# Stick-breaking attention by parts: the running product weighs differences of neighbouring value rows

## The chip, the cores and the metric

The kernel runs on one core of one Trainium2 chip. The metric is the device time of one execution in microseconds, lower is better. A core has a matrix engine (PE, with its weight loads shown apart as PEld), a vector engine (DVE), a scalar engine (ACT), a general engine (POOL) and an engine that here only issues DMAs (SP). PE, DVE, ACT and POOL each take their own instructions in a fixed order and wait for one another by semaphores. SBUF is the on-chip memory of tiles; PSUM is the small memory that matmuls write to. POOL works on SBUF alone.

## The reference, cut to what matters

One layer of a residual trunk: 2048 positions of width 1024. A combined projection gives four heads of differential attention and eight heads of stick-breaking attention, then an output projection and a SwiGLU feed-forward part follow. The change concerns the stick-breaking heads (width 64):

```python
z = jnp.einsum('bqhd,bkhd->bhqk', qb, k).astype(jnp.float32) * scale
mask = (k_pos[None, :] < q_pos[:, None])[None, None]
log_1mb = jnp.where(mask, jax.nn.log_sigmoid(-z), 0.0)
rem = lax.cumsum(log_1mb, axis=3, reverse=True) - log_1mb
a = jnp.where(mask, jnp.exp(jax.nn.log_sigmoid(z) + rem), 0.0)
return jnp.einsum('bhqk,bkhd->bqhd', a.astype(v.dtype), v)
```

For query t and key s < t the weight is sigmoid(z_ts) times the product, over the keys j between s and t, of sigmoid(-z_tj). Write C_s for the product of sigmoid(-z_tj) over s <= j < t, and C_t = 1. Since sigmoid(z) = 1 - sigmoid(-z), the weight is C_(s+1) - C_s.

## The kernel before

The whole kernel is one function, `block`. Work is in tiles of 128 positions (16 of them, index `i` for queries, `t` for the projection). Eight head groups run one after the other: `g` 0 to 3 are the differential heads (`diff_attn`), `g` 4 to 7 hold two stick-breaking heads each (`sb_attn`, map `m` 0 and 1). While the attention of one group runs, the projection of the next is made beside it (`proj_stream`, `advance`); beside group 7, which has no next group, runs the output projection (`out_proj`). The feed-forward part comes last.

A stick-breaking stage (`stage_a`) is one query tile, one head and one block `b` of up to 1024 keys, blocks from right to left. It takes two SBUF tiles of the pool `z4` (nine buffers, line 265): `be` for the weights and `om` for the running product. Per chunk of up to 512 keys, from right to left, these things happen:

- PE writes scores into a PSUM tile `sc` (four buffers; line 507). On the diagonal chunk one more matmul adds the mask (line 509), through a constant `tri` whose upper part is -1e38.
- ACT makes sigmoid(-z) into `om` (line 619) and sigmoid(z) into `be` or back into `sc` (line 620).
- DVE scans `om` in place from right to left, a running product that starts from 8192 or from the carry of the chunk to the right (line 622). The scan takes a second input, which its second operation passes by: the PSUM tile `sc`.
- The product of sigmoid(z) with the scan shifted by one key goes to `be` (line 623): on DVE with one input in PSUM, or, for the chunk `c == 1` of groups 4 to 6, on POOL (`aside`).

Then `split_t` (line 450) makes two 16-bit parts of the stage's weights, the high part by a cast on ACT (`to16`, line 89) and the rest by a subtraction on POOL (`tt`, line 98), and a DMA transposes both into `aT`. Some stages later (`PD`, `lag`) PE multiplies `aT` with the value rows (`pv`, line 518), three matmuls of 64 columns for each 128 keys, and accumulates in PSUM (`yp`). `finish` normalises and stores.

Values come from the projection. In groups 4 to 6 (`turned`) two tiles at a time are projected into two PSUM banks of the pool `psj`, which has two, and `split_psum` (lines 358 to 364) makes 16-bit high and low parts of the values in `v`, the high part on ACT or DVE by whichever has less noted load, the low part on DVE. Group 7 does the same tile by tile in `proj_out`.

The order of instructions on each engine is fixed when the program is built, by a scheduler that goes by priorities (`PRI`) and by what each instruction needs; nothing in the change touches its tables.

Of the kernel before, what the change touches and what calls it, by code (L numbers as in the profile page):

```python
# [11 lines left out]
F32 = mybir.dt.float32  # L12
# [17 lines left out]
HIDDEN = -1.0e38  # L30
# [29 lines left out]
def block(tc, a, out):  # L60
# [3 lines left out]
    with top:  # L64
# [54 lines left out]
        id16 = cp.tile([P, P], F16, name="id16")  # L119
        DVE.tensor_copy(id16[:], id32[:])  # L120
        idb = cp.tile([P, P], BF16, name="idb")
        DVE.tensor_copy(idb[:], id32[:])
        tri = cp.tile([P, P], BF16, name="tri")
        DVE.memset(tri[:], 0.0)
        POOL.affine_select(tri[:], tri[:], pattern=[[-1, P]], compare_op=ALU.is_gt, fill=HIDDEN, base=0, channel_multiplier=1)
# [131 lines left out]
        with ExitStack() as ph1:  # L257
# [4 lines left out]
            bias = s16p.tile([P, 4, 256], F32, name="bias", bufs=1)  # L262

# [21 lines left out]
            def load_w(g, st=None):  # L285
# [24 lines left out]
                else:  # L310
                    G["epsy"], G["kz"], G["nkz"] = c1(), c1(), c1()
                    DVE.tensor_scalar(G["epsy"][:], t2[:], EPS * 2.0 ** 28, 1e-37, op0=ALU.mult, op1=ALU.max)
                    times(kap, kap, kap)
                    DVE.tensor_scalar(G["kz"][:], kap[:], 2.0 ** -9, 2.0 ** -110, op0=ALU.mult, op1=ALU.max)
                    DVE.tensor_scalar(G["nkz"][:], G["kz"][:], -1.0, None, op0=ALU.mult)
                G["q"], G["k"], G["v"] = [], [], []
# [29 lines left out]
            def turned_out(pq, pv, qT, kT, v, j):  # L346
# [8 lines left out]
                vv = v[:, two, :].rearrange("p t (h s e) -> p t h s e", h=2, s=2)  # L355
                split_psum(vv[:, :, :, 0, :], vv[:, :, :, 1, :], pv[:, :256].rearrange("p (t h e) -> p t h e", t=2, h=2), 256)

            def split_psum(hi, lo, src, n):
                sc = 2.0 ** -11
                if pick(A=0.84 * n + 60, D=1.05 * n + 70) == "A":  # L360
                    ACT.mul(hi, src, sc)
                else:
                    DVE.tensor_scalar(hi, src, sc, None, op0=ALU.mult)
                DVE.scalar_tensor_tensor(lo, src, sc, hi, op0=ALU.mult, op1=ALU.subtract)  # L364
                note("D", 1.05 * n + 70)

            @pri("po")
            def proj_out(g, G, pj, B, j):
                st, v, raw = B
                nv = 1 if g < 4 else 2  # L370
                vv = v[:, j, :].rearrange("p (h s e) -> p h s e", h=nv, s=2)
                split_psum(vv[:, :, 0, :], vv[:, :, 1, :], pj[:, 256:384].rearrange("p (h e) -> p h e", h=nv), 128)
                if g < 4:
                    if pick(A=270, D=335) == "A":
# [3 lines left out]
                else:  # L378
                    split_psum(st[:, 0:4, j, 0, :], st[:, 0:4, j, 1, :], pj[:, :256].rearrange("p (c e) -> p c e", c=4), 256)

# [36 lines left out]
            def proj(g, G, fresh=None):  # L417
                for t in range(NT):
# [6 lines left out]
                    if t % 4 == 0:  # L425
                        v = sp.tile([P, 4, 256], F16, tag="v", bufs=KB, name=nm("v"))
                    if turned(g):
# [8 lines left out]
                        if t % 2 == 1:  # L436
                            turned_out(pq, pv_, qT, kT, v, t % 4)
# [6 lines left out]
                    proj_out(g, G, pj, (st, v, raw), t % 4)  # L444
# [59 lines left out]
            def score_chunk(G, sc, i, q, m, w, cut=False, turned=False):  # L504
# [3 lines left out]
                if cut:  # L508
                    last = PE.matmul(sc[:, 128 * w - P : 128 * w], lhsT=idb[:], rhs=tri[:], start=False, stop=True, skip_group_check=True)
# [3 lines left out]
            def pv(G, yp, y0, aT, b, n, o, wd, start, stop):  # L513
                nb = n // P
                for j in range(nb):
                    v = G["v"][2 * b + j // 4][:, j % 4, :]
# [79 lines left out]
            def sb_attn(g, G):  # L596
# [6 lines left out]
                def stage_a(i, m, b):  # L603
                    L = (i + 1) * 128
                    n = min(1024, L - 1024 * b)
                    be, om = z4(), z4()
                    if b == i // 8:
                        DVE.memset(om[:, n : n + 1], 8192.0)
                    else:
                        DVE.tensor_copy(om[:, n : n + 1], last[m][:, 0:1])  # L610
# [735 lines left out]
```

## Time and profile before

| what | value |
|---|---|
| three timed runs | 2677.06, 2681.61, 2683.46 us (median 2681.61) |
| span of the profiled execution | 2680.8 us (its own time is shown by this span alone) |
| differential groups 0 to 3, up to the first scan | 0 to 604 us |
| stick-breaking groups 4, 5, 6, first scan to last | 604 to 764, 764 to 923, 923 to 1094 us |
| stick-breaking group 7 with the output projection | 1094 to 1354 us |
| rest of the output projection | 1354 to 1427 us |
| feed-forward part | 1427 us to the end |

The profile is one execution on the chip. For a group of instructions it names the line, the engine, the operation, what is written and read, the count, the busy time and mean duration, and after a second bar the idle time of the engine just before them with what ended it. PE's busy time counts each matmul from issue to its last result, so matmuls overlap in it; the spacing of matmuls in a row tells what one costs.

### The profile page before, as it was taken

The page shows a single profiled execution, that of the slowest core. Times are in us where ns is not written, and L with a number is a line of the kernel's source. Part 1 is how long each engine was busy: PE and PEld are TensorE (multiplying, and loading weights), DVE is VectorE, ACT ScalarE, POOL GpSimd, SP SyncE. Part 2 cuts the span into 40 slices and gives each one's busy share as a digit, 9 for nine tenths or more (in the row PEclk, how much of TensorE's full clock was granted, in tenths as well). Part 3 has the DMA queues.
Part 4 walks back from the last instruction along what each step waited for, and adds up shares of the span by engine and source line. Part 5 has one row for each costly group of instructions (what it writes and reads, how often), then busy time and mean ns, then how long its engine had stood idle before and what let it go on. Part 6 is the DMA issues. An engine that isn't in the chain of part 4 may idle for free. (4 is left out here: it accounts for less than half of the span.)

```text
span 2680.8 us, 50579 instructions
## 1 busy us (share of the span) xinstructions
PE 2492.4 (93%) x19628; PEld 1498.6 (56%) x19628; DVE 1932.7 (72%) x3711; ACT 1347.0 (50%) x2487; POOL 1489.1 (56%) x1098
## 2 busy tenths in 40 slices
PE   6998989888988989889989899999999999999999
PEld 4655656577776776557775344444444444444444
DVE  6898969898989989877766868777685544444434
ACT  4665656567978878665644535344352112111121
POOL 2578667667767766546764656565564232322323
PEclk9999999999999999999999899999999999999999
DMA  6777697767998979987897574665649743635532
GB/s 222 213 162 181 146 200 168 179 143 184 193 179 179 185 160 209 210 191 217 218 285 282 208 250 178 255 226 202 245 183 346 293 177 143 233 141 186 195 111 95
DMA packets 619585, 534.41 MB, mean 199 GB/s; under 512 B 480640, under 2 KB 548224, under 8 KB 609104
## 3 DMA queue, kind: packets, MB, share of 16 engines
q1 hardware_dynamic: 617520, 529.09, 69.9%
q8 instruction: 154, 2.52, 0.4%
q0 software_dynamic: 512, 1.36, 0.2%
q14 instruction: 87, 0.71, 0.1%
q10 hardware_dynamic: 1312, 0.72, 0.1%
HBM read 261.08 MB, written 147.32 MB: 152 GB/s over the span
## 5 line engine op out<-in xcount | busy, mean ns | idle before, releaser
L98 POOL TENSOR_TENSOR s<-z,s 128x1024 f16<-128x1024 f32 (+7 forms) x288 | 472.0, 1647 | 142.5 <-ACT s L89 109.8
L507 PE MATMUL sc<-kT,qT 128*128 128x512 f16 (+3 forms) x1520 | 382.0, 353 | 53.3 <-DVE z L623 19.3
L622 DVE TENSOR_TENSOR_SCAN z<-z,sc 128x512 f32<-128x512 f32 (+3 forms) x320 | 352.8, 1112 | 58.6 <-ACT sc L620 38.0
L1138 PE MATMUL pd<-wd,act 128*128 128x512 f16 x1764 | 390.9, 379 | 1.2 <-DVE cg L1071 1.2
L326 PE MATMUL pj<-w,xt 128*128 128x384 f16 x1920 | 352.2, 331 | 18.8 <-ACT xt L683 6.9
L1030 PEld LDWEIGHTS <-wg 128*128 128x128 f16 x1848 | 182.0, 99 | 230.2 <-issue 16.4
L518 PE MATMUL yp<-v,aT 128*128 128x64 f16 (+1 forms) x4896 | 269.8, 204 | 41.6 <-DMA aT<-s 40.2
L518 PEld LDWEIGHTS <-aT 128*128 128x128 f16 x4896 | 237.5, 99 | 120.4 <-DMA aT<-s 52.5
L1030 PEld LDWEIGHTS <-wu 128*128 128x128 f16 x1848 | 180.7, 98 | 218.0 <-issue 2.6
L98 POOL TENSOR_TENSOR act<-cg,act 128x512 f16<-128x512 f32 x112 | 148.5, 1337 | 262.9 <-ACT act L1097 150.8
L1138 PEld LDWEIGHTS <-act 128*128 128x128 f16 x1764 | 172.8, 98 | 209.4 <-issue 2.8
L326 PEld LDWEIGHTS <-xt 128*128 128x128 f16 x1920 | 187.3, 99 | 147.5 <-issue 21.4
L89 ACT CAST s<-z 128x128 f16<-128x128 f32 (+7 forms) x215 | 173.1, 809 | 134.1 <-DMA aT<-s 40.5
L98 POOL TENSOR_TENSOR hs<-hs,cu 128x512 f32<-128x512 f32 x99 | 130.9, 1328 | 171.3 <-DVE hs L1144 70.8
L619 ACT ACTIVATE z<-sc,c 128x512 f32<-128x512 f32 (+3 forms) x320 | 210.7, 663 | 25.6 <-PE sc L507 11.7
L1097 ACT CAST act<-cg 128x512 f16<-128x512 f32 x126 | 77.3, 616 | 238.4 <-DVE cg L1103 162.7
L507 PEld LDWEIGHTS <-qT 128*128 128x128 f16 x1520 | 128.4, 99 | 121.0 <-DVE z L623 23.0
L832 PE MATMUL po<-wo,mt 128*128 128x256 f16 x1536 | 180.7, 277 | 13.9 <-DVE xf L835 8.4
L1030 PE MATMUL pm<-X,wu 128*128 128x512 f16 x792 | 180.4, 379 | 1.3 <-DVE wu L221 1.3
L1030 PE MATMUL pm<-X,wg 128*128 128x512 f16 x792 | 181.3, 382 | 0.0
L342 PE MATMUL pj<-xt,w 128*128 128x128 f16 x2304 | 175.0, 220 | 6.7 <-DVE v L364 5.7
L1144 DVE SCALAR_TENSOR_TENSOR hs<-pd,c,hs 128x512 f32<-128x512 f32 x136 | 99.0, 747 | 109.6 <-PE pd L1138 83.1
(266 smaller groups left out, 4737.6 us busy)
## 6 DMA issues: line engine op xcount, KB each, us to landing
xt<-xs SPq DMA_DIRECT2D x112, 512.0 KB, 4.3
hs<-hd SPq DMA_DIRECT2D x68, 512.0 KB, 4.5
hd<-hs SPq DMA_DIRECT2D x56, 512.0 KB, 4.7
split<-wg SPq DMA_DIRECT2D x11, 1792.0 KB, 7.8
split<-wu SPq DMA_DIRECT2D x11, 1792.0 KB, 6.7
split<-wd SPq DMA_DIRECT2D x11, 1792.0 KB, 7.2
wg<-split SPq DMA_DIRECT2D x11, 1792.0 KB, 7.3
wd<-split SPq DMA_DIRECT2D x11, 1792.0 KB, 12.2
```

Of the source, the lines that this page charges most:

```text
L89: ACT.copy(dst, src)
L98: (DVE if e == "D" else POOL).tensor_tensor(dst, a_, b_, op)
L326: PE.matmul(pj[:, :384], lhsT=xv[:, xi, kt, :], rhs=G["w"][:, wi, kt, :], start=n == 0, stop=n == 23)
L342: PE.matmul(o, lhsT=x_ if c == 2 else w_, rhs=w_ if c == 2 else x_, start=n == 0, stop=n == 23)
L507: last = PE.matmul(sc[:, : 128 * w].rearrange("p (t n) -> p t n", n=P), lhsT=G["q"][i // 4][:, a_, i % 4, :], rhs=G["k"][q][:, b_, 0:w, :] ...
L518: PE.matmul(yp[:, y0 : y0 + wd], lhsT=aT[:, a_, :], rhs=v[:, v_ : v_ + wd], start=start and j == 0 and q == 0, stop=stop and j == nb - 1 a ...
L619: ACT.activation(om[:, lo:hi], sc[:, :w], AF.Sigmoid, scale=G["nkz"][:])
L622: DVE.tensor_tensor_scan(ov, ov, sc[:, :w], om[:, hi : hi + 1], op0=ALU.mult, op1=ALU.bypass)
L832: PE.matmul(po[:, sl], lhsT=mt[:, kt, P * xi : P * xi + P], rhs=wos[2 * h + n][wi][:, kt, :], start=q == 0, stop=q == 23)
L1030: front[0] = PE.matmul(ps_[:].rearrange("p (t n) -> p t n", n=P), lhsT=wv[:, wo, wi, 128 * kt : 128 * kt + 128], rhs=X[xo][:, :, xi, kt, : ...
L1138: front[0] = PE.matmul(po[:], lhsT=act[:, ao, xi, 128 * j : 128 * j + 128], rhs=W["d"][:, wo, wi, :], start=start and u == 0 and q == 0, s ...
L1144: DVE.scalar_tensor_tensor(dst, po[:], kd[:], src, op0=ALU.mult, op1=ALU.add)
```

## The change

The sum over keys of (C_(s+1) - C_s) v_s is taken by parts: it is v_t plus the sum over s <= t of C_s (v_(s-1) - v_s), where in the kernel's scaling 8192 stands for 1. So the running product itself becomes the weight, and what it weighs is the difference of neighbouring value rows.

- The second sigmoid, the product with the shifted scan, the mask matmul and the carry column go. Only query tile `i == 0` keeps the old way, with raw values.
- On the diagonal chunk the scan multiplies and adds: its second input is a constant `diag`, zero but for 8192 on the diagonal, which starts the running product anew there. On other chunks the second input is `om` itself, passed by as before. The carry is a column of the neighbouring `om`.
- `steps_out` is new. It splits the projected values into 16-bit parts in a `z4` tile (`G["r"]`, two tiles per group, eight tiles of positions each), makes the differences with matmuls against the constants `dif` and `edge` into the same PSUM bank, and splits those into `v`.
- `stage_c` adds 8192 times the row's own value with two matmuls against the constant `idc`.

```diff
-                G["q"], G["k"], G["v"] = [], [], []
+                G["q"], G["k"], G["v"], G["r"] = [], [], [], []
...
-                vv = v[:, two, :].rearrange("p t (h s e) -> p t h s e", h=2, s=2)
-                split_psum(vv[:, :, :, 0, :], vv[:, :, :, 1, :], pv[:, :256].rearrange("p (t h e) -> p t h e", t=2, h=2), 256)
-
-            def split_psum(hi, lo, src, n):
-                sc = 2.0 ** -11
+                steps_out(G, pv, 256, 2, v, t)
...
+            def steps_out(G, pv, o, k, v, t):
+                t0 = t + 1 - k
+                r = t0 % 8
+                rv = G["r"][t // 8][:].bitcast(F16)[:, 256 * r : 256 * (r + k)].rearrange("p (t h s e) -> p t h s e", t=k, h=2, s=2)
+                split_psum(rv[:, :, :, 0, :], rv[:, :, :, 1, :], pv[:, o - P * k : o].rearrange("p (t h e) -> p t h e", t=k, h=2), P * k)
+                d = pv[:, o : o + P * k].rearrange("p (t h e) -> p t h e", t=k, h=2)
+                PE.matmul(d, lhsT=dif[:], rhs=rv[:, :, :, 1, :], start=True, stop=False, skip_group_check=True)
+                for u in range(max(t0, 1), t + 1):
+                    for s in range(2):
+                        PE.matmul(d[:, u - t0], lhsT=edge[:], rhs=raw_v(G, u - 1)[:, :, s, :], start=False, stop=False, skip_group_check=True)
+                PE.matmul(d, lhsT=dif[:], rhs=rv[:, :, :, 0, :], start=False, stop=True, skip_group_check=True)
+                vv = v[:, t0 % 4 : t0 % 4 + k, :].rearrange("p t (h s e) -> p t h s e", h=2, s=2)
+                split_psum(vv[:, :, :, 0, :], vv[:, :, :, 1, :], d, P * k, 1.0)
...
-                if cut:
-                    last = PE.matmul(sc[:, 128 * w - P : 128 * w], lhsT=idb[:], rhs=tri[:], start=False, stop=True, skip_group_check=True)
...
-                    be, om = z4(), z4()
-                    if b == i // 8:
-                        DVE.memset(om[:, n : n + 1], 8192.0)
-                    else:
-                        DVE.tensor_copy(om[:, n : n + 1], last[m][:, 0:1])
+                    om = z4()
+                    carry = 0.0 if b == i // 8 else last[m][:, 0:1]
...
-                        aside = c == 1 and turned(g)
-                        beta = be[:, lo:hi] if aside else sc[:, :w]
-                        ACT.activation(om[:, lo:hi], sc[:, :w], AF.Sigmoid, scale=G["nkz"][:])
-                        ACT.activation(beta, sc[:, :w], AF.Sigmoid, scale=G["kz"][:])
                         ov = om[:, lo:hi][:, ::-1]
-                        DVE.tensor_tensor_scan(ov, ov, sc[:, :w], om[:, hi : hi + 1], op0=ALU.mult, op1=ALU.bypass)
-                        (POOL if aside else DVE).tensor_tensor(be[:, lo:hi], beta, om[:, lo + 1 : hi + 1], ALU.mult)
+                        ACT.activation(om[:, lo:hi], sc[:, :w], AF.Sigmoid, scale=G["nkz"])
+                        DVE.tensor_tensor_scan(ov, ov, diag[:, 512 - w :][:, ::-1] if cut else ov, carry, op0=ALU.mult, op1=ALU.add if cut else ALU.bypass)
+                        carry = om[:, lo : lo + 1]
...
-                    return n, split_t(be[:, :n], n, "A", "P", wide[0] if g < NG - 2 else None)
+                    return n, split_t(om[:, :n], n, "A", "P", wide[0] if g < NG - 2 else None)
...
+                    if b == 0 and i > 0:
+                        for s in range(2):
+                            PE.matmul(yp[:, y0 : y0 + 64], lhsT=idc[:], rhs=raw_v(G, i)[:, m, s, :], start=False, stop=r == k - 1 and m == 1 and s == 1, skip_group_check=True)
```

What stands on DVE in group 5 for the left key block of query tile 14 shows the scans. Before (line 622 is the scan, 623 the product, 494 a part of `finish`; `z` are the `z4` tiles, `sc` the score banks):

```order
L622 SCALAR_TENSOR_TENSOR z_14308<-z_14308,sc_14310 128x512
L622 SCALAR_TENSOR_TENSOR z_14308<-z_14308,sc_14318 128x512
L623 TENSOR_TENSOR z_14307<-sc_14318,z_14308 128x512
L622 SCALAR_TENSOR_TENSOR z_14356<-z_14356,sc_14358 128x512
L494 SCALAR_TENSOR_TENSOR mo_14013<-yp_13017,c_269,mo_14013 128x4x128
L608 MEMSET z_14523 128x1
L622 SCALAR_TENSOR_TENSOR z_14356<-z_14356,sc_14366 128x512
L623 TENSOR_TENSOR z_14355<-sc_14366,z_14356 128x512
```

The same place on DVE with the change (the scan is line 638 now; 510 is a part of `finish`):

```order
L638 SCALAR_TENSOR_TENSOR z_13910<-z_13910,diag 128x384
L638 SCALAR_TENSOR_TENSOR z_13910<-z_13910 128x512
L638 SCALAR_TENSOR_TENSOR z_14033<-z_14033,z_13877 128x512
L638 SCALAR_TENSOR_TENSOR z_14033<-z_14033 128x512
L638 SCALAR_TENSOR_TENSOR z_14077<-z_14077,z_13910 128x512
L510 TENSOR_TENSOR y_13737<-yp_12812,yrs_13741 128x512
L638 SCALAR_TENSOR_TENSOR z_14077<-z_14077 128x512
```

The products are gone, scans follow one another, and no scan names a score bank any more: what it reads is its own tile, `diag`, or a neighbour's carry column.

On POOL the same stages stood like this before (line 623 is the product set aside, line 98 the low part of the 16-bit split):

```order
L623 TENSOR_TENSOR z_14307<-z_14307,z_14308 128x512
L623 TENSOR_TENSOR z_14355<-z_14355,z_14356 128x512
L98 TENSOR_TENSOR s_14199<-z_14179,s_14199 128x896
L98 TENSOR_TENSOR s_14326<-z_14307,s_14326 128x1024
L623 TENSOR_TENSOR z_14479<-z_14479,z_14480 128x512
```

And with the change:

```order
L98 TENSOR_TENSOR s_13890<-z_13877,s_13890 128x896
L98 TENSOR_TENSOR s_13923<-z_13910,s_13923 128x896
L98 TENSOR_TENSOR s_14046<-z_14033,s_14046 128x1024
L98 TENSOR_TENSOR s_14090<-z_14077,s_14090 128x1024
L98 TENSOR_TENSOR s_14216<-z_14203,s_14216 128x1024
```

POOL's row of splits is unbroken now; each split still needs the whole scan of its stage and its cast.

68 lines of the change are left out of this document (43 added, 25 removed).

## The prediction

> **What bounds the kernel now.** I read the page's first two parts, then the table of stages, then the groups of one stage, and last single tiles and stretches of time.
>
> ```profile
> span 2680.8 us, 50579 instructions
> PE 2492.4 (93%) x19628; PEld 1498.6 (56%) x19628; DVE 1932.7 (72%) x3711; ACT 1347.0 (50%) x2487; POOL 1489.1 (56%) x1098
> 604.00:764.00 160.00, 143.16 (x2216) 116.06 (x2214) 147.63 (x254) 139.10 (x259) 123.43 (x92) 1.00 0.90 185
> 764.00:923.00 159.00, 141.83 (x2247) 114.42 (x2245) 144.56 (x250) 132.65 (x241) 116.74 (x88) 1.00 0.96 185
> 923.00:1094.00 171.00, 152.04 (x2084) 114.28 (x2080) 150.72 (x267) 131.67 (x238) 117.36 (x90) 0.97 0.91 188
> 1094.00:1354.00 260.00, 228.85 (x2362) 178.01 (x2363) 202.82 (x355) 165.84 (x305) 145.92 (x101) 0.95 0.85 207
> 1427.00:2680.00 1253.00, 1228.74 (x5760) 566.23 (x5758) 740.17 (x1060) 396.88 (x517) 548.28 (x400) 0.99 0.56 205
> ```
>
> The five stage rows give the length, then the busy time of PE, PEld, DVE, ACT and POOL, the granted clock, and the DMA's share and GB/s. The first four are the stick-breaking groups 4 to 7, cut where the scans of one group end and the next begin; the change lives there. The last is the feed-forward part: PE is busy 98% of it, the change does not touch it, and I leave it alone. In groups 4 to 6 no engine is at its end by itself, but four are near it: in group 5 DVE is busy 144.6 of 159 us (91%), PE 141.8, ACT 132.7, POOL 116.7. DVE is the nearest to a bound. Group 5 stands for all three in what follows.
>
> ```profile
> L622 DVE TENSOR_TENSOR_SCAN z<-z,sc 128x512 f32<-128x512 f32 (+3 forms) x81 | 89.4, 1114 | 11.6 <-ACT sc L620 5.7 <-ACT z L620 3.9 <-DVE z L608 0.2
> L623 DVE TENSOR_TENSOR z<-sc,z 128x512 f32<-128x512 f32 (+3 forms) x48 | 29.5, 617 | 2.0 <-POOL s L98 0.5
> L610 DVE COPY z<-z 128x1 f32<-128x1 f32 x16 | 2.0, 144 | 0.0
> L608 DVE MEMSET z<- 128x1 f32 x32 | 1.8, 59 | 0.0
> L363 DVE TENSOR_SCALAR v<-pj 128x256 f16<-128x256 f32 x6 | 2.4, 404 | 0.0
> L364 DVE SCALAR_TENSOR_TENSOR v<-pj,v 128x256 f16<-128x256 f32 x8 | 3.3, 414 | 0.1
> L98 POOL TENSOR_TENSOR s<-z,s 128x1024 f16<-128x1024 f32 (+7 forms) x49 | 78.5, 1610 | 12.3 <-ACT s L89 12.0
> L623 POOL TENSOR_TENSOR z<-z,z 128x512 f32<-128x512 f32 (+3 forms) x33 | 30.6, 929 | 30.0 <-DVE z L622 26.4 <-DVE c L176 1.7 <-DVE z L608 1.6
> L220 POOL TENSOR_SCALAR w<-wst,sW 128x1536 f16<-128x1536 f32 x2 | 3.1, 1548 | 0.0
> L620 ACT ACTIVATE sc<-sc,c 128x512 f32<-128x512 f32 (+3 forms) x49 | 31.3, 639 | 0.0
> L620 ACT ACTIVATE z<-sc,c 128x512 f32<-128x512 f32 (+3 forms) x32 | 21.4, 668 | 0.0
> ```
>
> **The change part by part, in group 5.** *Removed from DVE:* the products, 29.5 us, and the carry copies and fills, 2.0 + 1.8: 33.3 us. *Added to DVE:* the differences are split once more, at most as much as the value split costs now, 2.4 + 3.3 = 5.7 us. DVE's own work becomes 144.6 - 33.3 + 5.7 = 117.0 us: 89.4 of scans and 27.6 of the rest. *ACT* loses the second sigmoid, 31.3 + 21.4 = 52.7 of 132.7 us. *POOL* loses the products set aside, 30.6 of 116.7 us. The scan's waits for the second sigmoid (the 5.7 and 3.9 above) go too, since a scan then needs the first sigmoid alone.
>
> *What is late next* depends on one thing that the diff shows and no time does: the scan. It read one tile of SBUF (om) and one of PSUM (sc). Now it reads om twice, or om and diag: both inputs in SBUF. These rows show what that costs beside a busy POOL (for a tile: count, then shortest, middle and longest ns):
>
> ```profile
> L98 DVE TENSOR_TENSOR cg<-cg,cg x66: 679/1224/1673, 1477.5 to 2625.7; 128x512 f32<-128x512 f32 x66
> L1047 DVE TENSOR_TENSOR cg<-pm,cg x22: 676/678/692, 1436.2 to 2591.7; 128x512 f32<-128x512 f32 x22
> L622 DVE TENSOR_TENSOR_SCAN z<-z,sc x320: 448/1270/1282, 603.7 to 1353.3; 128x512 f32<-128x512 f32 x91, 128x256 f32<-128x256 f32 x24, 128x384 f32<-128x384 f32 x24, 128x128 f32<-128x128 f32 x21
> L98 DVE TENSOR_TENSOR cu<-cg,cg x22: 675/691/1641, 1476.8 to 2623.4; 128x512 f32<-128x512 f32 x22
> 1765.55 1.16 POOL L98 TENSOR_TENSOR act<-cu,act 128x512 f16<-128x512 f32 x1 [1.28 <-ACT act L1097]
> 1765.65 1.60 DVE L98 TENSOR_TENSOR cg<-cg,cg 128x512 f32<-128x512 f32 x1
> 1766.67 1.60 POOL L98 TENSOR_TENSOR act<-cg,act 128x512 f16<-128x512 f32 x1
> 1767.29 1.53 DVE L98 TENSOR_TENSOR cg<-cg,cg 128x512 f32<-128x512 f32 x1
> ```
>
> The same operation on the same 512 columns takes 676 to 692 ns when one input is in PSUM (L1047), and anything from 679 to 1673 when both are in SBUF (L98). Today's scan never exceeds 1282. The last four rows show why: POOL works from 1765.55 to 1766.71; a DVE instruction issued at 1765.65 ends at 1767.25, 0.54 us after POOL; the next POOL one ends at 1768.27, 1.02 us after that; the next DVE one at 1768.82, 0.55 us after POOL. They take turns: neither streams while the other does. The Trainium skill, page "SBUF — State Buffer", section "Who interferes with whom", has it as a rule: a DVE instruction with two SBUF inputs contends with a GpSimd one that reads SBUF, and the second to come waits for the whole first one. The rows agree, and by the rule the change is a loss on DVE, where the diff alone promises a gain.
>
> *The price.* The four instructions took 3.27 us in all; alone they are 2 x 1.16 + 2 x 0.69 = 3.70, so each hides 0.11 us of its own start. If the scans take turns in the same way, group 5 has 89.4 of scans, 78.5 of splits and 3.1 of weight splits to put one after the other, less 0.11 for 132 instructions: 171.0 - 14.5 = 156.5 us. DVE's other 27.6 us can run beside POOL, but not beside a scan. Ends: all of it hides, 156.5 us (2.5 less than now); none does, 184 (25 more). A split follows on 49 of 81 scans, so I take 60% as hidden: 156.5 + 0.4 x 27.6 = 167.5, about 9 us more than now. The scan's own pace with both inputs in SBUF is not shown either; the nearest rows (678 with PSUM, shortest 675 and 679 without) say no difference, and I take none. The Trainium skill's "VectorE: DVE Perf Modes", errata section, gives a PSUM source 62 cycles more than an SBUF one; by that estimate 81 scans would save 5 us a group, which the rows just named do not show.
>
> *PE.* Each pair of value tiles adds two matmuls of 256 columns and four of 128, each row and head two of 64; the mask's 128 columns per row and head go.
>
> ```profile
> 1408.46 18.71 PE po L832 x170
> 841.51 0.63 PE L518 MATMUL yp<-v,aT 128*128 128x64 f16 x16
> 841.98 0.44 PE L342 MATMUL pj<-xt,w 128*128 128x128 f16 x5
> L342 PE MATMUL pj<-xt,w 128*128 128x128 f16 x754 | 54.9, 219 | 2.5 <-DVE v L364 1.6 <-POOL z L623 0.9
> L509 PE MATMUL sc<-tri,idb 128*128 128x128 bf16 x33 | 7.2, 219 | 0.0
> ```
>
> Back to back, 256 columns take 0.11 us, 128 take 0.055 and 64 some 0.03. So a group gains 8 x (0.22 + 0.22) + 60 x 0.03 = 5.3 us and loses 32 x 0.055 = 1.8: +3.5 us. By the same spacings PE's real work in a group is 1152 x 0.055 for the projection, 34816 x 3 columns of scores at 0.43 ns, and 816 x 0.03: about 133 us, then 137. Behind taking turns it is hidden; if the turns cost nothing, it is the bound. The projection's bank is also held longer, by a second pair of splits and the difference matmuls between (some 2 us). The wait there now is 1.6 us in this group; with eight pairs it lies between nothing and 16 us. A pair comes every 20 us, of which 5.3 are its own matmuls, so attention matmuls cover it: nothing. Buffers: one z4 tile per stage instead of two, but up to four hold raw values, so five stages fit where four and a half did: nothing. No DMA is added.
>
> *Group 7.*
>
> ```profile
> L623 DVE TENSOR_TENSOR z<-sc,z 128x512 f32<-128x512 f32 (+3 forms) x80 | 47.8, 603 | 1.9 <-DVE z L622 0.5
> L622 DVE TENSOR_TENSOR_SCAN z<-z,sc 128x512 f32<-128x512 f32 (+3 forms) x80 | 88.6, 1112 | 25.5 <-ACT sc L620 24.7
> L98 POOL TENSOR_TENSOR s<-z,s 128x1024 f16<-128x1024 f32 (+7 forms) x49 | 80.9, 1658 | 76.6 <-ACT s L89 57.7 <-issue 15.2 <-DVE x L98 2.6
> ```
>
> DVE loses 47.8 of 202.8 us. POOL is busy 145.9 of 260 us, 56%; if that share of 80 scans waits for half of a 1.66 us split, 37 us come back. What remains, 11 us, is not on a bound engine: I take nothing, within 15 either way.
>
> **Sum.** Three groups at +9 us: 27. The profiled span, 2680.8 us, is 0.8 below the median of the three runs (2681.6) and within their spread; the page shows no time around the span, so I add the 27 to the median: **2708 us**.
>
> **Rivals.** *(1) Faster: the scan takes no turns.* If a scan whose second input is only passed by, or is the same tile, does not hold POOL up, DVE has 117 us, and the place of the bound goes to PE's 137. At the 91% at which DVE runs now that is 151 us; at PE's 98% of the feed-forward part, 140. So 8 to 19 us a group, say 11, and 10 in group 7 from its waits for the second sigmoid (24.7): 43 us, 2638. It decides from the point where DVE fits under PE: (137 - 27.6) / 81, a mean of 1350 ns per scan. For it: no row shows a scan with both inputs in SBUF. Against it: every two-input DVE form there stretches. *(2) No change: the turns fit.* They cost 156.5 us a group if DVE's rest always finds a split running; with the waits for sigmoid and score banks gone, groups stay at 157 to 161, and the time at 2681. For it: POOL idled 12.3 us before its splits, room to shift them.
>
> **Chances.** Slower, as forecast: 0.50. Turns fit: 0.23. No turns: 0.27. A measurement here tells 0.3%, 8 us, from no change; the second case lies within that but for a few of its chances, so faster 0.28, same 0.22, slower 0.50. Range: the forecast's upper end, three times 25, plus 15 in group 7, is 2771, and I leave its last part out: 2745. Below, the no-turns case reaches from 2638 to some 2615; 2632 leaves a little under half of it out.
>
> **What would show it.** The scan group's mean: 1.1 us as now (rival 1), or 1.5 and more with a longest near 3 (forecast). POOL's split mean above 1.7 us says the same from the other side. Stage lengths: 165 or more, 157 to 161, or 140 to 152. ACT must drop by some 50 us a group in every case. I am wrong altogether if the scan stretches but the stages shorten, for then the turns are not what ends last; or if PE stands long before the projection, for then the held bank, taken at nothing, is.

## The result and the profile after

| kernel | median us | lowest to highest | ratio to before, 95% interval |
|---|---|---|---|
| before | 2680.89 | 2677.06 to 2683.46 | |
| with the change | 2883.03 | 2880.36 to 2891.6 | 1.0762, 1.0742 to 1.0782 |

The change makes the kernel 202 us slower. The forecast was 27 us slower, with a range that ended at 2745. The sign was right, the size was not.

The table of stages of the changed kernel, cut as before (length, then busy time of PE, PEld, DVE, ACT and POOL, granted clock, DMA share, GB/s): groups 4 to 7, the end of the output projection, the feed-forward part.

```profile
614.00:829.00 215.00, 159.43 (x2186) 127.40 (x2185) 163.72 (x153) 99.00 (x180) 110.71 (x59) 0.88 0.65 132
829.00:1047.00 218.00, 162.43 (x2336) 131.09 (x2336) 159.10 (x153) 101.31 (x183) 104.04 (x54) 0.87 0.64 133
1047.00:1271.00 224.00, 170.43 (x2275) 127.63 (x2275) 161.58 (x173) 104.33 (x199) 112.65 (x57) 0.89 0.71 146
1271.00:1547.00 276.00, 232.42 (x2366) 178.89 (x2363) 194.66 (x240) 131.93 (x245) 150.35 (x89) 0.93 0.80 193
1547.00:1620.00 73.00, 62.22 (x572) 54.83 (x571) 39.60 (x62) 25.72 (x33) 33.87 (x24) 0.95 0.89 317
1620.00:2879.00 1259.00, 1234.24 (x5833) 572.76 (x5830) 740.99 (x1064) 396.34 (x517) 551.47 (x403) 1.00 0.56 205
```

Cut at the scans' own starts, the groups grew by 55, 60, 52 and 14 us; the first scan comes 10 us later, and what follows the last scan grew by 7. Together that is 198, the difference of the two spans. Now look along the row of group 5: 218 us long, and no engine is near that. DVE is busy 159 us (73%; it was 91%), PE 162 (74%), ACT 101, POOL 104. The DMA's share fell from 0.96 to 0.64. A stage that is longer while every engine has more room is one in which engines wait for each other.

The scan and its partner among the groups of instructions of head group 5:

```profile
L638 DVE TENSOR_TENSOR_SCAN z<-z 128x512 f32<-128x512 f32 x32 | 68.7, 2156 | 1.5
L638 DVE TENSOR_TENSOR_SCAN z<-z,diag 128x128 f32<-128x128 f32 (+3 forms) x32 | 36.4, 1158 | 11.6 <-ACT z L637 11.6
L638 DVE TENSOR_TENSOR_SCAN z<-z,z 128x512 f32<-128x512 f32 x16 | 28.0, 1752 | 0.0
L98 POOL TENSOR_TENSOR s<-z,s 128x1024 f16<-128x1024 f32 (+7 forms) x48 | 92.7, 1945 | 103.4 <-ACT s L89 85.1 <-issue 18.1
L637 ACT ACTIVATE z<-sc,c 128x512 f32<-128x512 f32 (+3 forms) x80 | 45.7, 625 | 11.5 <-PE sc L530 9.9 <-DVE z L646 1.6
```

The scan by tile, for the whole kernel (count, then shortest, middle and longest ns):

```profile
L638 DVE TENSOR_TENSOR_SCAN z<-z,diag x128: 397/957/2825, 613.9 to 1533.1; 128x128 f32<-128x128 f32 x32, 128x256 f32<-128x256 f32 x32, 128x384 f32<-128x384 f32 x32, 128x512 f32<-128x512 f32 x32
L638 DVE TENSOR_TENSOR_SCAN z<-z x128: 1249/1924/3204, 633.0 to 1543.1; 128x512 f32<-128x512 f32 x128
L638 DVE TENSOR_TENSOR_SCAN z<-z,z x64: 1252/1275/3145, 688.0 to 1541.8; 128x512 f32<-128x512 f32 x64
```

All that the forecast named for taking turns is there. The 80 scans of group 5 take 133 us where 81 took 89 (a mean of 1.66 us; 1.5 or more was forecast), the longest takes 3.2 us (near 3), and POOL's splits rose from 1610 to 1945 ns (above 1700). The shortest scan of 512 columns, 1249 ns, is as fast as before. The turns can be seen singly, in rows of DVE and POOL from a stretch of time in group 5 (start, us):

```profile
894.70 2.26 DVE L638 TENSOR_TENSOR_SCAN z<-z 128x512 f32<-128x512 f32 x1
895.84 3.04 POOL L98 TENSOR_TENSOR s<-z,s 128x1024 f16<-128x1024 f32 x1
896.88 2.27 DVE L638 TENSOR_TENSOR_SCAN z<-z,diag 128x128 f32<-128x128 f32 x1
```

The first scan ends at 896.96; POOL's split, issued before that, ends at 898.88; the next scan has 128 columns, which take 397 ns at the shortest, was issued at 896.88 and ends at 899.15, 0.27 us after POOL. In these three rows nothing stretches evenly: the split does most of its work behind the first scan, and the short scan all but stands still until the split is done.

But the turns are not all. What the engines of group 5 waited for (us in total, times, longest):

```profile
POOL s L98 <- ACT s L89: 85.1, 21, 25.4
DVE qT L356 <- ACT qT L355: 36.0, 15, 8.7
ACT s L89 <- DVE z L638: 30.9, 17, 4.0
ACT qT L355 <- PE pj L347: 28.6, 6, 8.7
PE pj L372 <- DVE z L385: 19.9, 5, 9.3
```

POOL once stood 25.4 us for a cast on ACT, DVE 8.7 for a piece of the next group's projection (`qT` is the projected query). The longest single waits of group 5 before were 3.6 us. Two stretches of time in the table of busy times show what goes on meanwhile:

```profile
857.00:875.00 18.00, 16.24 (x285) 15.79 (x284) 5.00 (x10) 5.01 (x12) 3.44 (x2) 1.00 0.61 141
967.00:990.00 23.00, 18.62 (x305) 18.17 (x302) 3.25 (x8) 6.37 (x13) 1.92 (x2) 0.93 0.37 99
```

And DVE's row of instructions in the second of them, with its idle time in brackets:

```profile
965.12 1.26 DVE L638 TENSOR_TENSOR_SCAN z<-z 128x512 f32<-128x512 f32 x1
974.47 0.48 DVE L356 SCALAR_TENSOR_TENSOR qT<-pj,half,qT 128x256 f16<-128x256 f32 x1 [8.10 <-ACT qT L355]
...
988.27 0.48 DVE L356 SCALAR_TENSOR_TENSOR qT<-pj,half,qT 128x256 f16<-128x256 f32 x1 [8.72 <-ACT qT L355]
...
990.35 1.28 DVE L638 TENSOR_TENSOR_SCAN z<-z,z 128x512 f32<-128x512 f32 x1
```

For 23 us, from 967 to 990, PE does almost nothing but the projection of group 6. No scores are made, so DVE has no scan from 966.4 to 990.35 and is busy 3.25 us, POOL 1.92. In the order of PE's instructions this is a row of 285 projection matmuls with no score matmul between. A row is counted from one score matmul to the next, whatever other matmuls stand in it. Counted so, the longest rows of the changed kernel have 285, 285, 262, 253 and 253 matmuls; before, 96, 95 and 89. Of the 3456 projection matmuls of groups 4 to 6 (`proj_turned`), 2458 stand in rows of more than 60, before 624. So there are two suspects: the turns, and the order of PE's instructions that the builder made for the changed kernel.

A count from the trace's records parts them. Every instant of group 5, from its first scan to the first of the next group, is put under one of three heads: a scan or POOL is running; neither is, but DVE does other work; neither DVE nor POOL runs.

| kernel | group 5 | scan or POOL running | DVE's other work outside that | neither |
|---|---|---|---|---|
| before | 158.8 | 142.3 | 10.5 | 6.0 |
| with the change | 218.4 | 155.2 | 16.6 | 46.7 |

The prediction's sum for group 5 was 156.5 + 11 = 167.5. Measured are 155.2 + 16.6 = 171.8, close to it, and 46.7 us more in which neither ran, for which the sum had no term.

### The profile page after: what moved, and what is told of

It is laid out like the page before. It is cut to its first block, busy times and chain, and to the rows that moved or that the text cites. A ratio compares the mean times of both kernels' runs of the same rounds, so it can differ in the third digit from the quotient of the medians.

```text
span 2879.4 us, 50295 instructions
## 1 busy us (share of the span) xinstructions
PE 2561.8 (89%) x19940; PEld 1549.1 (54%) x19940; DVE 1975.4 (69%) x3321; ACT 1220.3 (42%) x2260; POOL 1462.2 (51%) x988
## 4 chain that ended last, share of the span: by engine, by line
PE 39%; DVE 9%; issue 3%; ACT 2%; DMA 1%; POOL 1%; SPq 0%; DVEq 0%; POOLq 0%; ACTq 0%
PE pd L1163 14%; PE pm L1055 9%; PE pd L1055 6%; PE pa L1055 6%; PE po L857 2%; DVE z L638 2%; DVE wd L214 1%; DVE wu L214 1%; DMA aT<-s 1%; DVE wg L214 0%; DVE cg L1128 0%; PE fsc L988 0%; DVE cg L98 0%; POOL s L98 0%; DVE x L98 0%
## 5 line engine op out<-in xcount | busy, mean ns | idle before, releaser
L98 POOL TENSOR_TENSOR s<-z,s 128x1024 f16<-128x1024 f32 (+7 forms) x288 | 537.0, 1877 | 372.7 <-ACT s L89 313.5
L530 PE MATMUL sc<-kT,qT 128*128 128x512 f16 (+3 forms) x1520 | 394.1, 371 | 73.0 <-ACT z L637 56.6
L331 PE MATMUL pj<-w,xt 128*128 128x384 f16 x1920 | 361.1, 336 | 20.6 <-DVE v L385 10.9
L539 PE MATMUL yp<-v,aT 128*128 128x64 f16 (+1 forms) x4872 | 305.8, 208 | 43.4 <-DMA aT<-s 39.8
L539 PEld LDWEIGHTS <-aT 128*128 128x128 f16 x4896 | 270.9, 102 | 121.5 <-DMA aT<-s 53.9
L1163 PEld LDWEIGHTS <-act 128*128 128x128 f16 x1764 | 172.5, 98 | 209.5 <-issue 2.4
L331 PEld LDWEIGHTS <-xt 128*128 128x128 f16 x1920 | 189.5, 100 | 155.2 <-issue 36.0
L638 DVE TENSOR_TENSOR_SCAN z<-z 128x512 f32<-128x512 f32 x128 | 258.7, 2027 | 8.3 <-ACT z L637 0.7
L89 ACT CAST s<-z 128x256 f16<-128x256 f32 (+7 forms) x215 | 166.3, 783 | 229.7 <-DVE z L638 75.6
L637 ACT ACTIVATE z<-sc,c 128x512 f32<-128x512 f32 (+3 forms) x320 | 183.7, 627 | 39.9 <-PE sc L530 29.3
L347 PE MATMUL pj<-xt,w 128*128 128x128 f16 x2304 | 188.9, 229 | 10.4 <-issue 4.7
L347 PEld LDWEIGHTS <-w 128*128 128x128 f16 x2304 | 167.5, 103 | 21.8 <-issue 14.0
```

The costliest lines, as they stand in the source:

```text
L89: ACT.copy(dst, src)
L98: (DVE if e == "D" else POOL).tensor_tensor(dst, a_, b_, op)
L331: PE.matmul(pj[:, :384], lhsT=xv[:, xi, kt, :], rhs=G["w"][:, wi, kt, :], start=n == 0, stop=n == 23)
L347: PE.matmul(o, lhsT=x_ if c == 2 else w_, rhs=w_ if c == 2 else x_, start=n == 0, stop=n == 23)
L530: last = PE.matmul(sc[:, : 128 * w].rearrange("p (t n) -> p t n", n=P), lhsT=G["q"][i // 4][:, a_, i % 4, :], rhs=G["k"][q][:, b_, 0:w, :] ...
L539: PE.matmul(yp[:, y0 : y0 + wd], lhsT=aT[:, a_, :], rhs=v[:, v_ : v_ + wd], start=start and j == 0 and q == 0, stop=stop and j == nb - 1 a ...
```

## The experiments

Each kernel was timed beside the kernel before on the same chip (whose medians lay between 2679.8 and 2682.6); ratios are to those, with 95% intervals.

**Two cures and two controls.** Run 1 gives the kernel before the suspected input alone:

```diff
-DVE.tensor_tensor_scan(ov, ov, sc[:, :w], om[:, hi : hi + 1], op0=ALU.mult, op1=ALU.bypass)
+DVE.tensor_tensor_scan(ov, ov, ov, om[:, hi : hi + 1], op0=ALU.mult, op1=ALU.bypass)
```

> The kernel before, only that the scan takes its own SBUF tile as second input in place of the score bank. Theory turns (scan and POOL's SBUF reads take turns, and this carries most of the 202 us): scan mean 1500 ns or more and 2800 us or more. Theory order (turns cost some 25 to 50 us by themselves, the rest comes from projections that stand in long runs on PE): the scan stretches all the same, but 2700 to 2740 us. If the second input costs nothing: 2681 within 8.

Measured: 2835.57 us, ratio 1.0586 (1.0564 to 1.0609), 155 us slower by one operand. The row of group 5:

```profile
816.00:1024.00 208.00, 158.58 (x2263) 128.99 (x2260) 178.15 (x251) 135.87 (x243) 150.23 (x87) 0.89 0.67 141
```

Its scans, splits and set-aside products there:

```profile
L622 DVE TENSOR_TENSOR_SCAN z<-z 128x512 f32<-128x512 f32 (+3 forms) x81 | 123.3, 1533 | 21.5 <-ACT z L619 18.9 <-DVE z L608 0.2
L98 POOL TENSOR_TENSOR s<-z,s 128x1024 f16<-128x1024 f32 (+7 forms) x49 | 101.0, 2074 | 17.2 <-ACT s L89 17.2
L623 POOL TENSOR_TENSOR z<-z,z 128x512 f32<-128x512 f32 (+3 forms) x32 | 40.1, 1257 | 41.2 <-DVE z L622 31.4 <-DVE z L608 5.8 <-ACT sc L620 1.9
```

The arithmetic is the same and the second input is only passed by, yet scan, split and set-aside product all stretch (1114, 1610 and 929 ns before). Under the three heads group 5 reads 181.8 + 11.5 + 14.2. The turns are a cause by themselves. The time with a scan or POOL running is longer here than in the change, where POOL has no products.

Run 2 takes the input away from 192 of the changed kernel's 320 scans; the 128 diagonal ones need `diag`:

```diff
-DVE.tensor_tensor_scan(ov, ov, diag[:, 512 - w :][:, ::-1] if cut else ov, carry, ...
+DVE.tensor_tensor_scan(ov, ov, diag[:, 512 - w :][:, ::-1] if cut else sc[:, :w], carry, ...
```

> The changed kernel, with the score bank as second input of the 192 scans that pass it by; the 128 diagonal scans keep their SBUF constant. Theory turns: the 192 scans go back to 1.27 us, and at least half of the 202 us comes back: 2780 or less. Theory order: the long runs of projections stay (the order of the build has them still), so 2830 or more.

Measured: 2793.84 us, ratio 1.043 (1.0411 to 1.045): 89 us come back, not all. Group 5 is 191 us under the heads 128.3 + 15.2 + 47.5: the running time fell by 27 us, the time with neither stayed.

Run 3 leaves out the matmuls of the differences; the values are split twice from the projection:

```diff
-                PE.matmul(d, lhsT=dif[:], rhs=rv[:, :, :, 1, :], start=True, stop=False, skip_group_check=True)
...
-                PE.matmul(d, lhsT=dif[:], rhs=rv[:, :, :, 0, :], start=False, stop=True, skip_group_check=True)
```

> The changed kernel without the difference matmuls; values are split once more straight from the projection, so the weights meet plain values. Theory chain (PE stands for the second split, 20 us in group 5 alone, and what hangs behind it): 2820 or less. Theories turns and order: within 25 of 2883.

Measured: 2900.94 us, ratio 1.0824 (1.0802 to 1.0846). Slower, not faster: PE's wait of 19.9 us for the split before the differences goes, and the time with neither in group 5 is 55.2. This chain is not what ends last.

Run 4 changes nothing but two numbers of the builder's priorities, that of the projection's matmuls and that of the attention's stages. Both at 0 is called level below; the numbers of the kernel before give the order as built:

```diff
-PRI = {"sc": 0, ..., "pm": -200, ..., "at": 200, "ox": 0, "wm": 0}
+PRI = {"sc": 0, ..., "pm": 0, ..., "at": 0, "ox": 0, "wm": 0}
```

> The changed kernel with the priorities of attention and projection matmuls both at 0, so that projections stand among the scores in pieces of 72 matmuls or fewer, where the changed kernel has runs of up to 285. Theory order: 2790 or less. Theory turns: 2860 or more, with scans as long as before.

Measured: 2794.0 us, ratio 1.0436 (1.041 to 1.0462): 89 us come back by order alone. All of it is in groups 4 to 6, which are 16, 35 and 41 us shorter than in the change. The longest rows of projection matmuls are two of 144, then 72. Rows of more than 60 hold 3013 matmuls, more than in the change, so it is the longest rows and not this sum that tell the two orders apart. The row of group 5:

```profile
817.00:1001.00 184.00, 149.44 (x2342) 122.55 (x2340) 143.74 (x154) 102.20 (x185) 97.61 (x54) 0.94 0.82 161
```

And two of its waits:

```profile
POOL s L98 <- ACT s L89: 72.5, 28, 5.0
DVE qT L356 <- ACT qT L355: 14.8, 14, 2.6
```

POOL's longest wait is 5.0 us instead of 25.4. Under the heads: 155.8 + 12.5 + 15.0 = 183.3. The running time is that of the change (155.2), the turns are all still there; of the time with neither, 32 us are gone. So both suspects are real, and they sit under different heads.

**Do they add?** Run 5 puts both edits together. Run 6 takes the turns from the diagonal scans as well, in the order as built: the mask matmul comes back, the scan starts from 8192 and never reads `diag`, and the term of the own row becomes that of the tile's last row.

```diff
-            DVE.tensor_scalar(idc[:], id32[:], CUM, None, op0=ALU.mult)
+            DVE.tensor_scalar(idc[:], id32[:, P - 1 : P].to_broadcast([P, P]), CUM, None, op0=ALU.mult)
...
-                    carry = 0.0 if b == i // 8 else last[m][:, 0:1]
+                    carry = CUM if b == i // 8 else last[m][:, 0:1]
...
-DVE.tensor_tensor_scan(ov, ov, diag[:, 512 - w :][:, ::-1] if cut else ov, carry, ...
+DVE.tensor_tensor_scan(ov, ov, sc[:, :w], carry, op0=ALU.mult, op1=ALU.bypass)
```

Run 7 is run 6 with level priorities; run 8 is the kernel before with level priorities.

> The changed kernel with both cures at once: 192 of the 320 scans take the scores' bank as their second input (the 128 diagonal ones still read diag), and the projection's and attention's priorities are level, which spreads the projection's matmuls. Each cure alone gave 89 us back of 202. Theory A (two causes that add): 2883 - 89 - 89, about 2705, with groups 4 to 6 near 165. Theory B (one cause seen twice, say idle engines that either cure fills): the second cure adds little, 2770 to 2795. Theory C (each hides the other: with either gone the other engine still waits): below 2680, groups under 159.

> The changed kernel with no scan at all that reads SBUF twice, in the build's own order: the mask matmul on the diagonal is back, so the scan starts from 8192 and takes the scores' bank as second input everywhere, and the diagonal's term is 8192 times the tile's last value row (a selector of row 127 in place of the identity). Theory A: the 128 diagonal scans of the earlier run without turns still had theirs, so scans now come back to 1.1 us, splits to 1.6, and another 5 to 10 us a group go: 2765 to 2780; the long projection runs stay and hold the groups at 180 and more. If turns were the whole loss: below 2690.

> As the kernel without any turns, and with level priorities that spread the projection's matmuls. Both causes gone. Theory A: what the prediction's first rival described, DVE at 117 us and PE at 139 in a group: groups of 145 to 160, 2640 to 2690. If the groups stay above 170, there is a third cause in the change.

> The kernel before with the same level priorities, as a control: its projection runs are short in either order (longest 127 matmuls against 96). Theory A (the order costs by its long runs): no change, 2681 within 15 us. If level priorities help for a reason of their own: 30 us or more faster here too.

Measured: run 5 2722.76 us, 1.0139 (1.0107 to 1.0172); run 6 2757.07, 1.0271 (1.0238 to 1.0303); run 7 2705.65, 1.0085 (1.0056 to 1.0113); run 8 2688.96, 1.0018 (1.0004 to 1.0032). Run 5 is 18 us short of the sum of the two cures (2705) and far from "one cause seen twice" (2770 and more). Run 6 gains more than expected from the diagonal scans: 37 us below run 2. Run 7 is 16 us above the upper edge of what was expected, so something third is left. Run 8 says that level priorities have no merit of their own in sum: groups 4 to 6 keep their lengths within 1 us, the first scan comes 17 us later and group 7 is 15 us shorter.

The scans of run 6 by tile:

```profile
L642 DVE TENSOR_TENSOR_SCAN z<-z,sc x256: 390/1236/1282, 617.5 to 1424.9; 128x512 f32<-128x512 f32 x62, 128x384 f32<-128x384 f32 x24, 128x128 f32<-128x128 f32 x23, 128x256 f32<-128x256 f32 x19
```

Its splits in group 5, and the row of that group:

```profile
L99 POOL TENSOR_TENSOR s<-z,s 128x1024 f16<-128x1024 f32 (+7 forms) x49 | 78.3, 1608 | 89.3 <-ACT s L90 53.2 <-issue 35.5 <-POOL s L99 0.5
```

```profile
794.00:973.00 179.00, 153.26 (x2368) 124.27 (x2366) 115.97 (x154) 101.47 (x182) 86.98 (x55) 0.97 0.85 163
```

The same row of run 7:

```profile
793.00:949.00 156.00, 145.31 (x2366) 121.53 (x2363) 115.62 (x153) 101.99 (x182) 85.52 (x54) 0.99 0.96 185
```

In run 6, with one input in PSUM, no scan exceeds 1282 ns (the other 64, which start from a neighbour's column, reach 1280) and the splits are back at 1608. DVE is busy 116 us of 179, and POOL and DVE still wait. What is left over the kernel before is there with no turns in it. Under the three heads, with the turns and the long rows each there and away:

| group 5 | scan or POOL | DVE's other | neither |
|---|---|---|---|
| turns, order as built (the change) | 155.2 | 16.6 | 46.7 |
| turns, level (run 4) | 155.8 | 12.5 | 15.0 |
| no turns, order as built (run 6) | 117.1 | 14.5 | 47.5 |
| no turns, level (run 7) | 130.7 | 10.4 | 15.0 |

The last column goes by the order alone: 47 or 48 with the long rows, 15 without. The first goes by the turns: 25 to 38 us of group 5.

**Long rows or any unevenness?** Runs 9 to 12 are run 6 with other pairs of priorities (attention and projection: 50 and 0; 0 and 100; 0 and -100; -100 and 0).

> As the kernel without any turns (2757), attention priority 50, projection 0. In the built order the projection matmuls that stand between two score matmuls: longest 144, 143, 143, 110; what exceeds 30 in a run sums to 1022 (no turns with the order as built: longest 287, 255, 255, sum 1864; with level priorities: 144, 144, then 72s, sum 1739; before: 96, sum 646). Theory L (the longest runs cost, since the engines behind PE run dry only past some 20 us): 2700 to 2720. Theory E (everything over a short run costs): below level priorities' 2706, down to 2690.

> As the kernel without any turns, attention 0, projection 100: longest runs 144, 144, 113, 113, 79; sum over 30 is 969, the least of all. Theory L: about 2706, as level priorities. Theory E: the fastest of these, 2685 to 2700.

> As the kernel without any turns, attention 0, projection -100: longest runs 181, 181, 144, 144, 116; sum over 30 is 1019. Theory L: between the order as built and level priorities, 2715 to 2740. Theory E: 2690 to 2705.

> As the kernel without any turns, attention -100, projection 0: longest runs 144, 144, 91, 91, 72; sum over 30 is 1065. Theory L: 2695 to 2706. Theory E: 2690 to 2705. If one of these four comes under 2681, the change's arithmetic is worth having once turns and order are taken away.

| run | longest rows | excess over 30, summed over all rows | median us | ratio, interval |
|---|---|---|---|---|
| 6 (as built) | 287, 255, 255 | 1864 | 2757.07 | 1.0271, 1.0238 to 1.0303 |
| 11 | 181, 181, 144 | 1019 | 2725.17 | 1.0157, 1.0138 to 1.0176 |
| 12 | 144, 144, 91 | 1065 | 2717.72 | 1.0137, 1.0115 to 1.016 |
| 10 | 144, 144, 113 | 969 | 2716.18 | 1.0129, 1.011 to 1.0149 |
| 7 (level) | 144, 144, 72 | 1739 | 2705.65 | 1.0085, 1.0056 to 1.0113 |
| 9 | 144, 143, 143 | 1022 | 2705.44 | 1.0087, 1.0062 to 1.0111 |

The theory that everything over a short row costs (E) falls: run 7 has the second-largest sum and ties for the fastest, and run 10 with the least was to be 2685 to 2700. Longest rows order the first two places and not the rest: runs 10 and 12 came out 10 and 12 us above what L gave. So the one order with rows of more than 200 matmuls is 32 us and more slower than the others, and below 150 this measure tells nothing. Where the rows stand does not settle it either: the rows of 144 of runs 7, 10 and 12 lie at the head of group 4, those of 143 of run 9 inside groups 4 and 5, and run 9 is as fast as run 7. That the order costs is shown; that it costs by the length of its rows is not. No order tried brings the change under the kernel before.

**The saving alone.** Runs 13 and 14 take the kernel before and only remove: no second sigmoid, no product, one `z4` tile per stage, and the builder's notes of load for what is gone. There are no difference steps, and the scan reads the score bank as before.

```diff
-                    be, om = z4(), z4()
+                    om = z4()
...
-                        ACT.activation(beta, sc[:, :w], AF.Sigmoid, scale=G["kz"][:])
...
-                        (POOL if aside else DVE).tensor_tensor(be[:, lo:hi], beta, om[:, lo + 1 : hi + 1], ALU.mult)
```

> The kernel before with the second sigmoid and the product left out (the running product itself goes to the value matmul, so its weights are other ones); nothing is added, the scan reads the scores' bank, the order as built: longest projection runs 142, 142, 133, 132. It is the saving of the change without its price. Theory P (the three causes are turns, long runs and, for the last 23 us, the difference steps): 2650 to 2680. Theory Q (lighter DVE, ACT and POOL buy nothing, since PE is what the groups end on): 2680 to 2720.

> The same with level priorities (longest runs 127, then 72). Against the changed kernel without turns and with level priorities (2706) it lacks only the difference steps: the second split of the values, the difference and edge matmuls, the 8192 term. Theory P: 2660 or less, groups 4 and 6 near 155 and 160. Theory Q: within 10 of 2706, or of 2689, the kernel before with level priorities.

Measured: in the order as built 2713.98 us, 1.0131 (1.0104 to 1.0157); level 2665.97, 0.9943 (0.9924 to 0.9961). Taking work away, a fifth of DVE's and some of ACT's and POOL's, and adding none, made the kernel 33 us slower. Groups 5 and 6 are 8 and 21 us longer and what follows the last scan 16; groups 4 and 7 are 3 and 10 shorter. Its projection stands in longer rows (142, 142, 133; 2139 of 3456 in rows over 60), and the time with neither in group 5 goes from 6.0 to 30.1 us. So the order turns bad by the removal itself and needs neither turns nor differences for it. With level priorities the same removal gains 14 us over before, and 23 over run 8, which has the same priorities. The stage of group 5 suggests why not more:

```profile
777.00:933.00 156.00, 141.43 (x2258) 116.95 (x2257) 115.27 (x190) 97.89 (x172) 85.60 (x54) 0.98 1.00 187
```

DVE went from 144.6 to 115.3 us, POOL from 116.7 to 85.6, and the group from 159 to 156. PE is busy 141.4 us of these, as much as before: it is now the engine nearest its end (91%), and the DMA's share reads 1.00. Which of the two holds the group was not tried.

**The third piece.** Run 7 against run 14 is the price of the difference steps with neither turns nor rows of more than 144: 40 us. With them go two smaller things: the carry is read from the neighbour's tile and not from a copy, and query tile 0 keeps the old way. Runs 15 to 17 take parts of them from run 7.

> The changed kernel without turns and with level priorities (2706) without the matmuls of 8192 times the tile's last value row (240 of 64 columns in the four groups): that term is left out of the output. By the columns, 240 x 0.03 us, 7 us; with the idle time behind them in the trace, 16. Theory M (the difference steps cost by their work on PE): 2690 to 2699. Theory B (they cost by holding: the raw values take one or two of nine tiles of the z4 pool, the projection's bank is held longer): 2700 to 2708.

> The same kernel with the matmuls that make the differences left out (the values are split twice and are not differences; the 8192 term stays). Theory M: the matmuls are 8 x 0.44 us a group and the wait between the two splits, 2685 to 2695. Theory B: raw values still take their tiles, 2700 to 2708.

> The same kernel with the values made as before: one split into v, no raw copy, no difference matmuls; only the 8192 term stays of the added steps, and reads v. Theory M: as the run without the difference matmuls, 2685 to 2695. Theory B: 2666 to 2680, most of the 40 us between 2666 (no added step at all) and 2706 gone.

| kernel, level priorities, no turns | median us | ratio, interval | group 4 |
|---|---|---|---|
| all difference steps (run 7) | 2705.65 | 1.0085, 1.0056 to 1.0113 | 174.7 |
| without the 8192 term (15) | 2694.76 | 1.0058, 1.0036 to 1.0081 | 174.0 |
| without the difference matmuls (16) | 2705.16 | 1.0095, 1.0071 to 1.0119 | 175.4 |
| also without raw copy and second split (17) | 2687.89 | 1.0029, 1.0015 to 1.0042 | 158.4 |
| the saving alone (14) | 2665.97 | 0.9943, 0.9924 to 0.9961 | 157.4 |

The difference matmuls cost nothing that can be seen. The raw copy, with its second split and the one or two tiles that it holds of the nine, costs 17 us (16 against 17, intervals apart), nearly all in group 4. This can be the order once more: runs 7, 15 and 16 have two rows of 144 projection matmuls at the head of group 4, runs 14 and 17 one of 127. Split, tiles and order were not parted. The 8192 term reads 11 us, but the intervals of 7 and 15 overlap. From run 17 to run 14 are 22 us more, 15 of them in group 6 (172.5 against 157.8 us), where run 15, without the term, still takes 169.0; so the term is at most a part, and the rest was not taken apart.

## Why the prediction was wrong, by its own steps

- **The turns are right, mechanism and price.** Group 5 was to need 156.5 us for scans and POOL one after another; 155.2 were measured. The rows of another stage's `cg` tiles, from which it was worked out, carried over to the scan. That the sum is so close is partly luck, since two misses offset each other: the scans alone take 85.7 us and not 89.4 (run 6), and 7.6 us of small products on POOL (`yrs`, a part of `finish`) were left out. The rule of the Trainium skill, page "SBUF — State Buffer", section "Who interferes with whom", agrees with run 1 (155 us by one operand) and run 6 (all of it gone with one input in PSUM). Rival 1, whose condition was a scan that takes no turns, did not arise; nor did rival 2, by which groups stay at 157 to 161 us.
- **How much of DVE's other work hides: mis-sized a little.** 60% of 27.6 us was taken as hidden, leaving 11; DVE's other work came to 31.7 us, and 16.6 lay outside. That is 5.6 us in group 5.
- **The step that failed is what the sum leaves out.** "If the scans take turns in the same way, group 5 has 89.4 of scans, 78.5 of splits and 3.1 of weight splits to put one after the other": this is the length of the stage only if one of them always has work. The time in which neither ran grew from 6.0 to 46.7 us, two thirds of the group's growth of 60. The prediction bounded the waits of DVE and POOL on each other and priced PE by its sum of work ("about 133 us, then 137 ... it is hidden"); where PE's work stands in the order was given no term. Run 4 against the change, and run 7 against run 6, put 32 us of it each on the order, the one with the long rows of projection matmuls; run 13 against 14 (30.1 against 17.2) shows that the removal brings some of it by itself. The order is not all: run 4 still lies 86 us above the forecast. Its groups 4 to 6 are 39, 25 and 11 us longer than before, 75 where 27 were forecast, so group 5 did not stand for all three. The stretch ahead of the first scan, group 7 and the end add 36, for which the sum had nothing.
- **The held bank and the buffers, "nothing".** The held bank is right in effect: PE waits 19.9 us in group 5 for the split before the differences, more than the 16 of its upper bound, but without those matmuls nothing is gained (runs 3 and 16). On the buffers ("five stages fit where four and a half did: nothing") the runs leave it open: raw copy, second split and tiles together cost 17 us (run 17), mostly in group 4, and how much of that is the tiles was not parted.
- **Rival 1's price, 43 us gained, was wrong too.** Its condition was set up by run 7: no turns, and no rows of more than 144. It is 23 us slower than before, since the difference steps cost 40. Even the saving alone, run 14, gains only 14.
- **Group 7 held, at its edge and by luck.** Forecast within 15 of nothing, measured 14 us longer. Its terms did not hold: DVE's relief of 47.8 us shortened it by 10 (run 13), the turns took 18 and not 37 (the change against run 6), and the difference steps, at nothing, took 7 (run 6 against 13).
- **ACT's drop was mis-sized.** "ACT must drop by some 50 us a group in every case": it dropped by 31, from 132.7 to 101.3. The 52.7 us were the sum of the durations of two groups of instructions, and durations on ACT overlap: the groups named in the rows of before (52.8 and 39.9 beside 31.3 and 21.4) sum to 145 within 132.7 us of busy time.

```profile
L619 ACT ACTIVATE z<-sc,c 128x512 f32<-128x512 f32 (+3 forms) x80 | 52.8, 666 | 2.5 <-PE sc L507 1.8 <-PE sc L509 0.7
L89 ACT CAST s<-z 128x1024 f16<-128x1024 f32 (+7 forms) x48 | 39.9, 835 | 20.1 <-DMA aT<-s 5.6 <-DVE z L623 4.3 <-issue 3.3
```

Nothing hung on it, since ACT was not near its end.

The parts in order, each a difference of two medians. Before 2681; the saving alone 2714 (+33); the difference steps 2757 (+43); the turns 2883 (+126). With level priorities: 2689, 2666 (-23), 2706 (+40), 2794 (+88). The order costs nothing before (-8), 48 in the saving, 51 with the difference steps, and 89 once the turns are there. So turns and order do not simply add: 38 us of the 126 are there only with both.

Open stays why the builder makes the long rows; run 13 shows that it makes longer ones when the second sigmoid and the products go, and run 4 that two priorities undo them. Whether that is the lighter work, the second `z4` tile or the notes of load was not tried. Open stays also what most of the 22 us between runs 17 and 14 are. The granted clock in groups 4 to 6 fell to 0.87 to 0.89 with the change. In group 5 that goes along with the turns and not with the time in which neither ran: run 1 has turns, 14.2 us of neither and 0.89, run 6 no turns, 47.5 us and 0.97. What the clock itself costs was not tried apart.

## What to carry to other kernels

Before an operand of a vector instruction moves from PSUM to SBUF, ask what POOL does at that time: one passed-by operand cost 155 us here, and leaving it in PSUM cost nothing. A stage's length is not the sum over its bound pair: work taken from several engines can change the order in which a builder puts the rest, so read the order of the engine that feeds them too, and count the time in which none of the bound engines runs. An order tuned to the old balance is part of the kernel; try a lighter kernel with its priorities loosened before judging its arithmetic.

## What the runs showed of the hardware that was not expected

A scan whose second operand is its own tile, and whose second operation passes that operand by, still takes turns with POOL as if it read two tiles: in run 1 its longest took 3218 ns instead of 1282:

```profile
L622 DVE TENSOR_TENSOR_SCAN z<-z x320: 452/1384/3218, 602.0 to 1509.2; 128x512 f32<-128x512 f32 x89, 128x128 f32<-128x128 f32 x24, 128x384 f32<-128x384 f32 x24, 128x256 f32<-128x256 f32 x23
```

So the operand counts, not whether its value is used. A short scan pays for the wait like a long one: a scan of 128 columns, 397 ns at its shortest, took 2.27 us behind a split of 1024.
